# A transformer block on one core: the embedding's product moved to the prologue, roots on POOL, operands laid out in step

## The chip, the cores and the metric

The kernel runs on one core of a Trainium2 chip. The metric is the device time of one execution in microseconds (us), the median of several runs; less is better. The engines are named as in the profile: PE is TensorE (matmuls), DVE is VectorE, ACT is ScalarE, POOL is GpSimd, SP is SyncE, whose queue issues most of the DMAs. PEld is PE's loading of weights.

## The reference

One block on 512 tokens of width 1024, fp32 throughout. Cut to what matters:

```python
n1 = rmsnorm(x, g_mix)                       # x * rsqrt(mean(x*x) + 1e-6) * g
z = n1 @ w_in
y_ssm = s5_mixer(z[..., :512], ...)          # state-space mixer; its step sizes are dt = exp(log_dt)
y_nsa = nsa_mixer(z[..., 512:1024], z[..., 1024:1792], z[..., 1792:1816], ...)   # attention
merge = sigmoid(z[..., 1816:])
h = x + (merge_a * (y_ssm @ w_br_ssm) + merge_b * (y_nsa @ w_br_nsa)) @ w_out
h = h + conv_ffn(rmsnorm(h, g_ffn))          # up, depthwise conv, gelu(a) * b, down
gate = sigmoid(rmsnorm(h, g_ple) @ w_ple_gate)
h = h + gate * (p @ w_ple_proj)              # p is an input, 512 x 256
out = rmsnorm(h, g_final)
```

The embedding's product, `p @ w_ple_proj`, depends on inputs alone: it may be formed at any time before the last lines.

## The kernel before, in words

Every product is formed as three matmuls in a format that keeps the leading part of an fp32 number. An operand is split into a high part (a copy in that format, `copy`, L75) and a low part (what is left, a subtraction at L55; the pair is `split`, L78). `mm3` (L82 to L85) then sums high·high (L83), low·high (L84) and high·low (L85) in one PSUM bank. Tiles have 128 partitions; most matmuls write 128 x 512. Names ending in `h` and `l` are high and low parts; `wr` is a raw weight tile of 512 KB (three buffers), `wh` and `wl` its split (two buffers each).

The stages, by the time at which they stand in the trace before: the prologue (0 to 33 us); the state-space mixer and the projections `pj` of `n1` (from 33, with attention between and after them); the gated branches `glu` and `br`; the output product `wo` (to 404); the FFN's up products `ua` and `ub` (404 to 640) and its down products, formed with sums of blocks (`p`, to 770); last the PLE gate `pg` with the embedding's product, which also bears the name `pj` (767 to 824), the final norm and the output.

**The prologue.** SP loads the first tile of x, `g_mix`, the weights of the values and the attention's gates (`wv0`, `wv1`), the other three tiles of x, and two weights for u. For each tile of x the squares are summed (`squared`, L293; of the first tile ACT and DVE take half each), `rstd_of` (L121) turns the sum into a reciprocal root by eight dependent DVE operations of one or two columns (a first guess by bit pattern and three Newton steps), `x_scaled` multiplies by the root and by `gb`, the gain spread over partitions by a matmul with ones; `t_high` transposes on PE (`nt`) and copies the high part `n1h` on ACT, `t_low` subtracts to `n1l` on DVE; `v_passes` (L282) forms the values and gates (`vps`, 280 columns) in three passes of eight matmuls. The order of PE, ACT and DVE in this block is written by hand (the block under `manual_schedule`, L328). POOL's and SP's order is set by a scheduler; each engine's queue runs strictly in the order that it has been given.

POOL forms the mixer's parameters meanwhile: from `prm` (transposed parameters) the step sizes `dt`, an exponential of 22 small operations (`exp_of`, on POOL with a product and a sum as two instructions), then `lr`, `th`, `kk`, `fl`, a second exponential `rho`. DVE forms the angles `ang` and their sines later. POOL also clears the tiles `Z` and `CX` ahead of all this.

**The end.** `prepare` (L1278) is a generator whose steps are taken between products of the FFN's down stage: it loads p (`pin`), splits the weights of the gate, transposes p on PE (`ptr`, L1293) and splits it into `pTh`, `pTl`, loads `w_ple_proj` and splits it on POOL into `wph`, `wpl`. `embedded` (L1476) then forms one 128 x 512 tile of the embedding's product, six matmuls, in a PSUM bank; `gated` (L1482) forms the gate's product, a tanh on ACT (`sgt`), and on DVE adds gate times embedding to `hres`, the residual; ACT sums squares, POOL multiplies by the final gain, `rstd_of` gives the root, ACT and DVE scale the output.

Of the kernel before, what the change touches and what calls it, by code (L numbers as in the profile page):

```python
# [45 lines left out]
def hybrid_kernel(ctx: ExitStack, tc: tile.TileContext, A, out):  # L46
# [199 lines left out]
    xload(0)  # L246
    nc.sync.dma_start(grow, dr("g_mix", 0, [[D, 1], [1, D]]))
# [18 lines left out]
    ss4 = small("ss4", NQ + 1, 1)  # L266
# [25 lines left out]
    def squared(qt):  # L292
        S.activation(sq, xts[qt], AF.Square, accum_out=ss4[:, qt:qt + 1])  # L293
# [33 lines left out]

    with tc.manual_schedule(engines={mybir.EngineType.PE, mybir.EngineType.Activation, mybir.EngineType.DVE}):  # L328
        gbs = [bank("s", f"gb{i}") for i in range(2)]
        for ps, g in zip(gbs, halves(grow)):  # L330
            PE.matmul(ps, ones, g, start=True, stop=True)
        x0 = halves(xts[0])
        S.activation(sq[:, :512], x0[0], AF.Square, accum_out=ss4[:, 0:1])
        V.tensor_tensor_reduce(out=sq[:, 512:], in0=x0[1], in1=x0[1], scale=1.0, scalar=0.0, op0=MUL, op1=ADD,
                               accum_out=ss4[:, NQ:])
        pps = bank("t", "pps")
        for i in (2, 0, 1):
            PE.transpose(pps[:, i * 16:(i + 1) * 16], prow[:, i], ident[:NPAIR, :NPAIR])
        PE.transpose(pps[:, 48:52], drow, ident[:4, :4])
        copy(*wv(0, 0))  # L340
        copy(prm.rearrange("p a b -> p (a b)"), pps[:, :48])
        copy(dcol, pps[:, 48:52])
        x_scaled(0, rstd_of(ss4[:, 0:1], ss4[:, NQ:]))
        squared(1)
        t0 = t_high(0)
        V.tensor_copy(*wv(0, 1))
        v_passes(0, (0,))
        t_low(t0)
        v_passes(0, (1,))
        squared(2)  # L350
        squared(3)
        x_scaled(1, rstd_of(ss4[:, 1:2]))
        t1_ = t_high(1)
        v_passes(1, (0,))
        r = rstd_of(ss4[:, 2:4], n=2)
# [83 lines left out]
    exp_of(rho, lr, "e1", G)  # L439
# [158 lines left out]
    for t in (*ZZ[0], *CX[0], *ZZ[1], *CX[1]):  # L598
        G.memset(t, 0.0)
# [617 lines left out]
    with tc.manual_schedule(engines={mybir.EngineType.PE}):  # L1217
# [296 lines left out]
```

## Time and profile before

| | |
|---|---|
| median of 3 runs | 833.9 us (833.75 to 833.94) |
| the profiled execution: span | 833.0 us; some 0.9 us of a run lie outside the span |
| PE busy | 810.8 us, 97% of the span, 4535 instructions |
| DVE, ACT, POOL busy | 515.9, 391.3, 264.2 us |
| HBM | 75.54 MB read, 3.15 MB written |
| first projection matmul, last matmul | 33.0, 824.2 us |

How to read it: rows of a timeline give the start and the duration in us, engine, line, operation, the tile written, an arrow, the tiles read, and in brackets how long the engine was idle ahead of it and what ended that. Rows of windows give the stretch, its length, the busy time of PE, PEld, DVE, ACT and POOL with counts, the granted clock of PE as a share, the share of DMA engines that were busy, and GB/s. Rows with a count (x16) and three numbers are of one kind of instruction: least, median and greatest duration in ns. Matmuls overlap in their pipe: a 128 x 512 matmul lasts 389 ns, while the next starts after about 0.23 us.

### The profile page before, as it was taken

The numbers are of one execution on the slowest core, as the hardware profiler recorded it, in microseconds if no ns is written. First come the engines' busy times: TensorE is split into PE (matmuls) and PEld (weight loads), VectorE is DVE, ScalarE is ACT, GpSimd is POOL, SyncE is SP. The second block draws the span as 40 slices with busy tenths as digits, with TensorE's granted clock in tenths as the row PEclk, the third lists the DMA queues.
The fourth block names the chain that finished last, engine by engine and source line by source line (L and its number), as shares of the span: only waits on it lengthen the run. The fifth ranks groups of instructions, "written<-read, shape, count | busy, mean of one in ns | idle before, by whom it ended". The sixth has DMA issues, their size and how long they took to land. (4 is left out here: it accounts for less than half of the span.)

```text
span 833.0 us, 12232 instructions
## 1 busy us (share of the span) xinstructions
PE 810.8 (97%) x4535; PEld 678.6 (81%) x4535; DVE 515.9 (62%) x1067; ACT 391.3 (47%) x723; POOL 264.2 (32%) x320
## 2 busy tenths in 40 slices
PE   7999999999999999999999999999999999999995
PEld 5877888888888878888898888888888888877885
DVE  6899988377777641685454444445555755778643
ACT  4436553445777653434354444444444433546522
POOL 6585110124555533221033333333333000050311
PEclk9999999999999999999999999999999999999999
DMA  9653322422334413343053333333322553321011
GB/s 243 159 165 102 90 65 65 128 76 77 80 73 99 136 49 102 126 140 88 1 152 90 89 100 101 102 101 102 93 88 72 168 186 127 102 89 63 26 51 52
DMA packets 112001, 83.67 MB, mean 100 GB/s; under 512 B 9665, under 2 KB 97477, under 8 KB 111942
## 3 DMA queue, kind: packets, MB, share of 16 engines
q1 hardware_dynamic: 111262, 81.82, 33.9%
q10 hardware_dynamic: 680, 1.07, 0.3%
q8 instruction: 36, 0.59, 0.3%
q14 instruction: 23, 0.19, 0.1%
HBM read 75.54 MB, written 3.15 MB: 94 GB/s over the span
## 5 line engine op out<-in xcount | busy, mean ns | idle before, releaser
L55 POOL TENSOR_TENSOR wl<-wr,wh 128x1024 fp32r<-128x1024 f32 x39 | 93.6, 2400 | 246.9 <-ACT wh L76 228.9
L76 ACT ACTIVATE wh<-wr 128x1024 fp32r<-128x1024 f32 x92 | 97.3, 1059 | 95.8 <-issue 31.5
L55 DVE TENSOR_TENSOR wl<-wr,wh 128x1024 fp32r<-128x1024 f32 x53 | 68.4, 1291 | 49.2 <-ACT wh L76 49.2
L83 PE MATMUL pj<-n1h,wh 128*128 128x512 f32 x224 | 91.9, 410 | 0.4 <-ACT un L76 0.4
L85 PE MATMUL pj<-n1h,wl 128*128 128x512 f32 x224 | 88.8, 397 | 0.4 <-DVE wl L55 0.4
L84 PE MATMUL pj<-n1l,wh 128*128 128x512 f32 x224 | 88.8, 397 | 0.0
L64 DVE SCALAR_TENSOR_TENSOR cv<-ub,cvp,cv 128x511 f32<-128x511 f32 (+1 forms) x44 | 32.9, 748 | 65.5 <-ACT cv L1181 64.8
L84 PE MATMUL ua<-n2l,wh 128*128 128x512 f32 (+1 forms) x176 | 67.0, 381 | 0.4 <-DVE n2l L64 0.4
L83 PE MATMUL ua<-n2h,wh 128*128 128x512 f32 (+1 forms) x176 | 66.9, 380 | 0.2 <-ACT n2h L166 0.2
L83 PE MATMUL ub<-n2h,wh 128*128 128x512 f32 (+1 forms) x176 | 66.8, 379 | 0.0
L85 PE MATMUL ub<-n2h,wl 128*128 128x512 f32 (+1 forms) x176 | 66.8, 379 | 0.0
L84 PE MATMUL ub<-n2l,wh 128*128 128x512 f32 (+1 forms) x176 | 66.8, 379 | 0.0
L85 PE MATMUL ua<-n2h,wl 128*128 128x512 f32 (+1 forms) x176 | 66.7, 379 | 0.0
L85 PEld LDWEIGHTS pj<-n1h,wl 128*128 128x128 f32 x224 | 42.5, 190 | 10.3 <-DVE wl L55 1.1
L61 POOL TENSOR_SCALAR pr<-pr,su,gates 128x512 f32<-128x512 f32 (+1 forms) x64 | 38.4, 608 | 37.4 <-DVE su L877 36.3
L84 PEld LDWEIGHTS pj<-n1l,wh 128*128 128x128 f32 x224 | 42.6, 190 | 7.9 <-issue 0.6
L83 PEld LDWEIGHTS pj<-n1h,wh 128*128 128x128 f32 x224 | 42.5, 190 | 7.9 <-ACT un L76 0.6
L874 DVE CUSTOM_DVE_ANT_0 pr<-sps,maskb 128x512 f32<-128x512 f32 (+1 forms) x64 | 30.0, 487 | 18.8 <-PE sps L870 9.4
L55 DVE TENSOR_TENSOR pl<-ptp,ph 128x128 fp32r<-128x128 f32 (+1 forms) x64 | 31.1, 487 | 14.5 <-ACT ph L76 13.8
L76 ACT ACTIVATE ph<-ptp 128x128 fp32r<-128x128 f32 (+1 forms) x64 | 27.6, 433 | 25.7 <-PE ptp L885 25.0
L84 PEld LDWEIGHTS ua<-n2l,wh 128*128 128x128 f32 x176 | 33.1, 188 | 6.8 <-DVE n2l L64 0.6
L83 PEld LDWEIGHTS ua<-n2h,wh 128*128 128x128 f32 x176 | 33.1, 188 | 6.6 <-ACT n2h L166 0.5
(468 smaller groups left out, 2049.2 us busy)
## 6 DMA issues: line engine op xcount, KB each, us to landing
wr<-in_w_up_dram SPq DMA_DIRECT2D x44, 512.0 KB, 3.8
wr<-in_w_in_dram SPq DMA_DIRECT2D x28, 512.0 KB, 4.0
wr<-in_w_down_dram SPq DMA_DIRECT2D x12, 512.0 KB, 3.5
b<-in_w_down_dram SPq DMA_DIRECT2D x10, 512.0 KB, 4.0
QQ<-QT SPq DMA_DIRECT2D x16, 256.0 KB, 3.4
wr<-in_w_out_dram SPq DMA_DIRECT2D x8, 512.0 KB, 4.7
wr<-in_w_ple_gate_dram SPq DMA_DIRECT2D x8, 512.0 KB, 3.5
xall<-in_x_dram SPq DMA_DIRECT2D x4, 512.0 KB
```

What stands on the lines that cost most here:

```text
L55: e.tensor_tensor(o, a, b, op=op)
L61: e.tensor_scalar(o, a, s1, s2, op0=op0, op1=op1)
L64: e.scalar_tensor_tensor(o, a, s, b, op0=op0, op1=op1)
L76: S.activation(o, a, AF.Copy)
L83: PE.matmul(ps, lh, rh, start=start, stop=False)
L84: PE.matmul(ps, lh, rl, start=False, stop=False)
L85: PE.matmul(ps, ll, rh, start=False, stop=stop)
L874: V.tensor_tensor_reduce(out=pp, in0=ps[:, :w], in1=maskb[:, T - w:], scale=-(HD ** -0.5), scalar=3e38, op0=ADD, op1=ALU.min, accum_out=nb)
```

## The change

Its parts, in the order of the diff:

1. `rstd_of` has two POOL operations: the sum plus epsilon, then a power with exponent -0.5. The factor 1/1024 goes into the square's scale on ACT (`square`). All sums of squares lie in padded tiles (`sums`, `sums3`).
2. SP loads p first, then half of `w_ple_proj`, `g_mix`, x0, the other half, x1, `wv0`, x2, x3, `wv1`, the weights of u.
3. The prologue's hand-written order gets the whole embedding's product: p is transposed and split, `w_ple_proj` split, and eight tiles `eps` formed by `e_passes`, grouped by pass (first high·high of four tiles, so that it needs no low part) and put between the steps of x. ACT copies each tile to SBUF (`e_out`), SP writes it to a buffer in the HBM (`pjd`, 256 KB each).
4. The step sizes' exponential goes from POOL to DVE (14 operations there), the angles' reduction from DVE to POOL (12 operations of 128 x 128). `Z` and `CX` are cleared after the copy to `prow`. The squares of x0 are all ACT's.
5. `prepare` no longer transposes p nor splits `w_ple_proj`; it reads the eight tiles back from the HBM, and `gated` takes them from there. `embedded` is gone.
6. Small tiles are gathered or padded (`odds`, `sums`, `sums3`, two columns for `pe`) so that matmul operands start at the same place modulo 256 bytes of a partition: 224 bytes past a multiple in the build after, where the build before has 32, 160 and 224.

PE's queue at the program's start, before (`gb` is the gain spread, `nt` transposes of x, `vps` values):

```order
L331 MATMUL gb_141<-wv_110,ones 128x512
L331 MATMUL gb_142<-wv_110,ones 128x512
L338 MATMUL pps<-ident,prow 128x16 x3
L339 MATMUL pps<-ident,drow 128x4
L308 MATMUL nt<-ident,xall 128x128 x8
L282 MATMUL vps<-WV,n1h 128x280 x8
L282 MATMUL vps<-WV,n1l 128x280 x8
L308 MATMUL nt<-ident,xall 128x128 x8
L282 MATMUL vps<-WV,n1h 128x280 x8
L282 MATMUL vps<-WV,n1l 128x280 x8
L308 MATMUL nt<-ident,xall 128x128 x8
```

and after (`ptr` transposes of p, `eps` the embedding's tiles):

```order
L373 MATMUL ptr<-ident,pin 128x128 x8
L401 MATMUL pps<-ident,prow 128x16 x3
L402 MATMUL pps<-ident,drow 128x4
L384 MATMUL eps<-wh,pTs 128x512 x8
L411 MATMUL gb_192<-wv_112,ones 128x512
L411 MATMUL gb_193<-wv_112,ones 128x512
L384 MATMUL eps<-wl,pTs 128x512 x4
L384 MATMUL eps<-wh,pTs 128x512 x4
L384 MATMUL eps<-wl,pTs 128x512 x4
L384 MATMUL eps<-wh,pTs 128x512 x4
L343 MATMUL nt<-ident,xall 128x128 x8
L384 MATMUL eps<-wh,pTs 128x512 x4
```

The first transposes of x stand behind the transposes of p, 24 matmuls `eps` and `gb`; two more groups of 12 `eps` follow behind the first and the second tile's transposes. The value passes of the first tile, which stood right behind its transposes, now come behind those of the third.

DVE's root of the second tile of x, before (`ss` is the sum, `xall` x):

```order
L346 CAST WV<-wv_124 128x8x152
L55 TENSOR_TENSOR n1l<-nt,n1h 128x4x128 x2
L61 TENSOR_SCALAR rv_203<-ss_136 128x1
L61 TENSOR_SCALAR ry_204<-rv_203 128x1
L64 SCALAR_TENSOR_TENSOR rt_205<-ry_204,rv_203 128x1
L64 SCALAR_TENSOR_TENSOR ry_204<-rt_205,ry_204 128x1
```

and after, on POOL, in the midst of the mixer's parameters (`sums` holds the sums; `rv_277` and `ry_278` are the two operations of that root):

```order
L59 TENSOR_SCALAR gtFalse<-rd 128x16
L55 TENSOR_TENSOR at<-fl,mt 128x128
L55 TENSOR_TENSOR kk<-gtFalse,kk 128x16
L55 TENSOR_TENSOR ang<-kk,mt 128x128
L59 TENSOR_SCALAR gtFalse<-e1n 128x16
L61 TENSOR_SCALAR rv_277<-sums 128x1
L61 TENSOR_SCALAR aq<-ang 128x128
L59 TENSOR_SCALAR a_535<-ang 128x128
L55 TENSOR_TENSOR e1r<-gtFalse,e1x 128x16
L55 TENSOR_TENSOR ry_278<-rv_277,sums 128x1
```

The root's first half has 22 operations that follow from `dt` (rows from `lr` on, of which the first five shown are the last) ahead of it, and three other operations between its halves.

SP's queue at the start, before (`wv_110` holds `g_mix`, then the values' weights; `wv_124` their second part; `wr` weights of u):

```order
L244 DMA xall<-in_x_dram 128x1024
L247 DMA wv_110<-in_g_mix_dram 1x1024
L258 DMA wv_110<-in_w_in_dram 128x8x128
L258 DMA wv_124<-in_w_in_dram 128x8x152
L244 DMA xall<-in_x_dram 128x1024 x3
L183 DMA wr<-in_w_in_dram 128x8x128 x2
L263 DMA grow_113<-in_g_ffn_dram 8x128
```

and after (`wv_112` and `wv_134` are the two value tiles; the first two `wr` are halves of `w_ple_proj`):

```order
L251 DMA pin<-in_p_dram 128x4x256
L180 DMA wr<-in_w_ple_proj_dram 128x2x512
L261 DMA wv_112<-in_g_mix_dram 1x1024
L241 DMA xall<-in_x_dram 128x1024
L180 DMA wr<-in_w_ple_proj_dram 128x2x512
L241 DMA xall<-in_x_dram 128x1024
L270 DMA wv_112<-in_w_in_dram 128x8x128
L241 DMA xall<-in_x_dram 128x1024 x2
L270 DMA wv_134<-in_w_in_dram 128x8x152
L180 DMA wr<-in_w_in_dram 128x8x128
```

x0 stands behind p and half of `w_ple_proj`; x1 behind the other half, but ahead of the values' weights.

The diff, cut to its core:

```diff
     def rstd_of(ss, ss2=None, n=1):
-        v, y, t = (small(f"r{c}{n}", n) for c in "vyt")
-        ts(v, ss, 0.0 if ss2 is None else ss2, D * EPS, ADD, ADD)
-        ts(y.bitcast(I32), v.bitcast(I32), -0.5, FIRST, MUL, ADD)
-        for a in NEWTON[:3]:
...
+        v, y = (small(f"r{c}{n}", n) for c in "vy")
+        ts(v, ss, 0.0 if ss2 is None else ss2, EPS, ADD, ADD, G)
+        tt(y, v, minus[:, :n], ALU.pow, G)
         return y
...
+    def square(junk, x, acc):
+        S.activation(junk, x, AF.Square, scale=ROOT, accum_out=acc)
...
+    def p_turned(k):
+        ps = bank("t", "ptr")
+        for qt in range(NQ):
+            PE.transpose(ps[:, qt * P:(qt + 1) * P], pin[:, qt, k * P:(k + 1) * P], ident)
+        copy(pTs[:, 0, k], ps)
+        return ps
+
+    def e_passes(h2, qts, passes):
+        for n in passes:
+            for qt in qts:
+                if n == 0:
+                    eps[h2, qt] = bank(either(), "eps")
+                x, y = ((0, 0), (0, 1), (1, 0))[n]
+                for k in range(2):
+                    PE.matmul(eps[h2, qt], pTs[:, x, k, qt * P:(qt + 1) * P], wp[h2][y][:, k], start=n + k == 0,
+                              stop=n == 2 and k == 1)
+
+    def e_out(h2, qt):
+        t = stage[4 * h2 + qt]
+        if t is None:
+            t = pw.tile([P, 512], F32, name="pj", tag="mg")
+        copy(t, eps[h2, qt])
+        nc.sync.dma_start(pjd[h2, qt], t)
...
+        e_passes(0, range(4), (0,))
         gbs = [bank("s", f"gb{i}") for i in range(2)]
         for ps, g in zip(gbs, halves(grow)):
             PE.matmul(ps, ones, g, start=True, stop=True)
...
+        squared(0)
+        e_passes(0, range(2), (1, 2))
+        wp_tiles(1)
+        copy(wp[1][0], wpr[1])
+        exp_of(dt, prm[:, 2], "e0", V)
+        tt(wp[1][1], wpr[1], wp[1][0], SUB)
+        x_scaled(0, rstd_of(ss4[:, 0:1]))
+        e_out(0, 0)
+        e_out(0, 1)
+        squared(1)
+        e_passes(0, (2, 3), (1, 2))
+        e_out(0, 2)
+        e_out(0, 3)
+        t0 = t_high(0)
+        e_passes(1, range(2), (0, 1, 2))
+        x_scaled(1, rstd_of(ss4[:, 1:2]))
+        t_low(t0)
...
-            for k in range(2):
-                ps = bank(either(), "ptr")
...
-            for h2 in range(2):
-                raw = wraw("w_ple_proj", D, 0, h2 * 512, 2, 512)
-                for k in range(2):
-                    WP[k, h2] = [Slot(f"wp{x}", 1, F32R).t for x in "hl"]
-                    split(*WP[k, h2], raw[:, k], G)
...
+            for hf, qt in order:
+                pjs[hf, qt] = Slot("pj", 1).t
+                nc.sync.dma_start(pjs[hf, qt], pjd[hf, qt])
```

More of the change, by code (lines that the diff above doesn't have):

```diff
@@ L326, in u_split, with wp_tiles @@
             tt(uw[ct][1], uraw[ct], uw[ct][0], SUB)
-    with tc.manual_schedule(engines={mybir.EngineType.PE, mybir.EngineType.Activation, mybir.EngineType.DVE}):
+    pjd = pud.tile([2, NQ, P, 512], F32, name="pjd")
+    stage = [pin_[:, 1, :512], pin_[:, 1, 512:], pst[:, 0], pst[:, 1], None, None, pin_[:, 0, :512], pin_[:, 0, 512:]]
+    wp, eps = {}, {}
+    def wp_tiles(h2):
+        wp[h2] = [pw.tile([P, 2, 512], F32R, name=n, tag=n) for n in ("wh", "wl")]
+    def p_turned(k):
[19 more added lines that the diff above has]
+        nc.sync.dma_start(pjd[h2, qt], t)
+    with tc.manual_schedule(engines={mybir.EngineType.PE, mybir.EngineType.Activation, mybir.EngineType.DVE}):
+        wp_tiles(0)
+        pps_ = [p_turned(0)]
+        V.tensor_copy(wp[0][0], wpr[0])
+        pps_.append(p_turned(1))
+        pps = bank(either(), "pps")
+        for i in (2, 0, 1):
+            PE.transpose(pps[:, i * 16:(i + 1) * 16], prow[:, i], ident[:NPAIR, :NPAIR])
+        PE.transpose(pps[:, 48:52], drow, ident[:4, :4])
+        copy(prm.rearrange("p a b -> p (a b)"), pps[:, :48])
+        copy(dcol, pps[:, 48:52])
+        for k in range(2):
+            tt(pTs[:, 1, k], pps_[k], pTs[:, 0, k], SUB)
+        tt(wp[0][1], wpr[0], wp[0][0], SUB)
+        e_passes(0, range(4), (0,))
         gbs = [bank("s", f"gb{i}") for i in range(2)]
@@ L331, in hybrid_kernel @@
             PE.matmul(ps, ones, g, start=True, stop=True)
[L332 to L339, printed above, removed]
@@ L340, in hybrid_kernel @@
-        copy(*wv(0, 0))
[L341 to L355, printed above, removed]
@@ L1267, in onto @@
             tt(hres[:, qt, cs], hres[:, qt, cs], x, op, e)
-        WG, WP, pT, n3 = [], {}, {}, {}
+        WG, n3, pjs = [], {}, {}
+        order = [(hf, qt) for qp in range(2) for hf in range(2) for qt in (2 * qp, 2 * qp + 1)]
         def n3_(x, k, q, w):
@@ L1278, in prepare @@
         def prepare():
-            pin = pw.tile([P, NQ, PLE], F32, name="pin", tag="wr", bufs=3)
-            nc.sync.dma_start(pin, dr("p", 0, [[PLE, P], [P * PLE, NQ], [1, PLE]]))
             yield
@@ L1430, in hybrid_kernel @@
         sgn = [0]
-        ss = [pf.tile([P, 4], F32, name=f"ssf{qt}") for qt in range(NQ)]
-        def embedded(hf, qt):
-            qs_ = slice(qt * P, (qt + 1) * P)
-            pjs[hf, qt] = bank("s", "pj")
-            for k in range(2):
-                mm3(pjs[hf, qt], pT[k][0][:, qs_], pT[k][1][:, qs_], *WP[k, hf], k == 0, k == 1)
-        pjs = {}
+        ss = [sums3[:, 16 + 8 * qt:20 + 8 * qt] for qt in range(NQ)]
         def gated(hf, qt):
-            if (hf, qt) not in pjs:
-                embedded(hf, qt)
             pj = pjs[hf, qt]
@@ L1473, in gated @@
                         bass.AP(tensor=out.tensor, offset=out.offset + qt * P * D + i * 512, ap=[[D, P], [1, 512]]), o)
-        embedded(0, 0)
-        embedded(0, 1)
-        for n, (hf, qt) in enumerate([(hf, qt) for qp in range(2) for hf in range(2) for qt in (2 * qp, 2 * qp + 1)]):
+        for n, (hf, qt) in enumerate(order):
             if n in (2, 3):
```

167 lines of the change are left out of this document (91 added, 76 removed).

## The prediction

> **What bounds the kernel now.** I began with the page's busy times, then looked by windows for stretches in which TensorE is not full.
>
> ```profile
> PE 810.8 (97%) x4535; PEld 678.6 (81%) x4535; DVE 515.9 (62%) x1067; ACT 391.3 (47%) x723; POOL 264.2 (32%) x320
> 0.00:5.00 5.00, 0.10 (x1) 0.13 (x1) 0.37 (x1) 1.65 (x2) 4.36 (x26) 1.00 0.52 167
> 25.00:30.00 5.00, 4.06 (x32) 3.83 (x31) 4.36 (x5) 1.89 (x3) 4.33 (x7) 1.00 0.17 40
> 187.70:191.10 3.40, 3.40 (x10) 2.65 (x9) 3.40 (x7) 1.06 (x4) 2.83 (x2) 0.51 0.01 2
> 751.00:824.00 73.00, 72.06 (x358) 60.06 (x356) 46.55 (x108) 33.52 (x73) 14.11 (x10) 1.00 0.11 37
> 800.00:833.00 33.00, 24.50 (x131) 21.09 (x129) 13.04 (x38) 7.81 (x18) 6.58 (x6) 0.95 0.13 48
> ```
>
> The kernel is TensorE's queue from end to end: 97% busy. What it lacks lies at the start (x is awaited for 4.9 us), at the end (8.5 us after the last matmul) and in a few short waits. In 751 to 824, where the embedding's product stands now, TensorE has 72.06 of 73 us: a matmul taken out there shortens the run by its own time. The prologue is what has to pay for it, so I read TensorE's timeline there, with what released the first rows of other engines.
>
> ```profile
> 4.90 3.75 PE L331 MATMUL gb<-wv,ones 1*128 1x512 f32 x4 [4.90 <-DMA wv<-in_g_mix_dram]
> 8.91 1.97 PE L308 MATMUL nt<-ident,xall 128*128 128x128 f32 x8
> 22.83 1.14 PE L308 MATMUL nt<-ident,xall 128*128 128x128 f32 x8
> 24.84 1.19 PE L282 MATMUL vps<-WV,n1h 128*128 128x280 f32 x8
> 28.00 4.38 PE L282 MATMUL vps<-WV,n1h 128*128 128x280 f32 x32 [0.94 <-DVE WV L55]
> 33.01 0.48 PE L83 MATMUL pj<-n1h,wh 128*128 128x512 f32 x1
> 4.63 0.63 ACT L333 ACTIVATE sq<-xall 128x512 f32<-128x512 f32 x1 [0.56 <-DMA xall<-in_x_dram]
> 10.02 1.06 ACT L293 ACTIVATE sq<-xall 128x1024 f32<-128x1024 f32 x1 [0.73 <-DMA xall<-in_x_dram]
> ```
>
> The first projection matmul (`pj`, L83) starts at 33.01. From there on TensorE is nearly unbroken, so the change is settled by two numbers: how much later than 33.01 that matmul starts, and how much shorter the rest becomes. The transposes also show a slow start: 8 of them take 1.97 us at 8.91 and 1.14 at 22.83.
>
> **What the rest saves.** The embedding's product at the end, and the transposes of p that served it:
>
> ```profile
> 751.09 1.03 PE L1293 MATMUL ptr<-ident,pin 128*128 128x128 f32 x8
> 751.88 0.48 PE L83 MATMUL p<-wh,s14x 128*128 128x512 f32 x1
> 817.68 0.39 PE L85 MATMUL pj<-wph,pTl 128*128 128x512 f32 x1
> 818.37 0.39 PE L85 MATMUL pj<-wph,pTl 128*128 128x512 f32 x1
> L83 PE MATMUL pj<-wph,pTh x16: 389/389/478, 767.4 to 817.9; 128*128 128x512 f32 x16
> ```
>
> Between 817.68 and 818.37 lie three matmuls, 0.23 us each. Three passes of 16 are 48, so 11.0 us; the transposes hold the queue from 751.09 to 751.88, 0.8; changing tiles adds some 0.2. **12.0 us** go. What comes back is eight reads of 256 KB at a DMA share of 0.11, which I cost at nothing; if they came late, each would hold up the DVE step behind `sgt`, which isn't TensorE's.
>
> Beside it the splits of `w_ple_proj` on POOL go, and those of p on DVE:
>
> ```profile
> 747.51 1.71 POOL L55 TENSOR_TENSOR hres<-hres,su 128x512 f32<-128x512 f32 x1
> 748.02 2.35 DVE L55 TENSOR_TENSOR wl<-b,wh 128x512 fp32r<-128x512 f32 x2
> 749.82 0.50 PE L84 MATMUL p<-wl,s23x 128*128 128x512 f32 x1 [1.72 <-DVE wl L55]
> 752.56 0.69 DVE L55 TENSOR_TENSOR wl<-b,wh 128x512 fp32r<-128x512 f32 x1
> ```
>
> TensorE waits 1.72 us for a `wl` pair that takes 2.35 beside a POOL addition, where one alone takes 0.69. POOL is late there because `wpl` splits lie between its additions. With them gone I take **1.5 us** back (bounds 0 and 1.9).
>
> Roots: today eight dependent DVE operations, then two on POOL.
>
> ```profile
> 826.47 0.21 DVE L61 TENSOR_SCALAR rv<-ssf 128x1 f32<-128x1 f32 x1 [0.64 <-ACT sq L1459]
> 826.52 0.72 POOL L55 TENSOR_TENSOR hres<-hres,g 128x256 f32<-128x256 f32 x1 [1.98 <-ACT sq L1459]
> 828.43 0.72 ACT L1471 ACTIVATE xf<-hres,ry 128x512 f32<-128x512 f32 x1 [1.99 <-issue]
> 17.71 0.22 POOL L55 TENSOR_TENSOR lr<-lre,dt 128x16 f32<-128x16 f32 x1
> 23.35 0.25 POOL L59 TENSOR_SCALAR gtFalse<-e1n 128x16 f32<-128x16 f32 x1
> 411.55 0.39 PE L83 MATMUL ua<-n2h,wh 128*128 128x256 f32 x1 [0.24 <-ACT n2h L166]
> ```
>
> The DVE chain lasts 1.96 us (826.47 to 828.43). Nineteen small POOL operations last from 17.71 to 23.35, 0.30 each, so two are 0.6. No row shows a power; its near end is 0.30, its far end what an addition of 512 columns takes at its slowest above, 1.71. I take 0.3 to 0.4, since it writes one column as the nineteen write sixteen. At the tail POOL first does its `hres` (826.52, 0.72) and only then the root: 827.9 in place of 828.43, **0.4 us**. Ahead of the FFN some 1.2 us of chain go, of which TensorE shows a wait around 411: **0.7**. The SSM's tables lose twelve operations of DVE to POOL; two waits there are TensorE's, and with the queues between and behind them some 2.6 us, of which I take **1.5** (bounds 0 and 2.6):
>
> ```profile
> 62.05 0.50 PE L83 MATMUL pj<-n1h,wh 128*128 128x512 f32 x1 [0.36 <-ACT un L76]
> 69.89 1.16 PE L648 MATMUL wps<-Uc,WB 128*128 128x128 f32 x8 [0.89 <-ACT WB L76]
> ```
>
> Operands in step. In the build of before, `n2h`, `n2l` and `wh` start 32 bytes past a multiple of 256, `y`, `ys`, `mTh`, `w0h` 224 past, `oS` and `w1l` 160 past; after, all are 224 past. The rows, read by those phases:
>
> ```profile
> L83 PE MATMUL ua<-n2h,wh x176: 278/389/396, 404.7 to 641.9; 128*128 128x512 f32 x160, 128*128 128x256 f32 x16
> L83 PE MATMUL wo<-w0h,mTh x32: 387/389/499, 358.4 to 398.3; 128*128 128x512 f32 x32
> L84 PE MATMUL glu<-ys,wh x16: 390/394/398, 165.3 to 175.9; 128*128 128x512 f32 x16
> L85 PE MATMUL br<-oS,wl x32: 392/398/398, 337.0 to 358.2; 128*128 128x512 f32 x32
> ```
>
> Equal phases give 389 ns (32 with 32 in `ua`, 224 with 224 in `wo`), unequal ones 394 to 398. The unequal 512-wide ones are 48 of `glu`, 192 of `br` (in two tiles, `y` as `glu`) and, by half, some 100 of `wo`: 240 × 6 ns + 100 × 3 ns = **1.7 us** (bounds 0 and 2.5, and below nothing in a rival). [...]
>
> Together 12.0 + 1.5 + 0.4 + 0.7 + 1.5 + 1.7 = **17.8 us**.
>
> **What the prologue costs.** The walk of the new order, as an estimate. Before, four loads of 512 KB lie between x0 (4.6) and x1 (10.0), 1.3 to 1.8 each. Now p comes first (4.9), then half of `w_ple_proj` (6.2), x0 (7.5), the other half, x1 (10.1). TensorE: transposes of p to 6.6, pass 0 of four tiles, 8 matmuls at twice 0.23 while slow, 7.0 to 10.4; gb, its 3.75 at most, to 13.8.
>
> ```profile
> 9.35 0.81 DVE L346 CAST WV<-wv 128x1216 fp32r<-128x1216 f32 x1
> 12.89 0.14 DVE L61 TENSOR_SCALAR rv<-ss 128x1 f32<-128x1 f32 x1
> 14.65 1.41 DVE L64 SCALAR_TENSOR_TENSOR xall<-xall,ry,gb 128x512 f32<-128x512 f32 x2
> 26.64 1.38 POOL L55 TENSOR_TENSOR e1q<-gtFalse,e1r 128x16 f32<-128x16 f32 x1
> 27.87 1.24 DVE L55 TENSOR_TENSOR wl<-wr,wh 128x1024 fp32r<-128x1024 f32 x1
> ```
>
> DVE's queue: from 6.2 the cast, 0.8, two `pTs` 1.3 (each 0.69 as the subtraction at 752.56, overlapping a little), `wl` 1.2, to 9.5; the 14 dependent operations of the step sizes at 0.22 to 0.24 (eight take 12.89 to 14.65) to 12.8; `wl` to 14.0; x0 scaled 1.4, to 15.4. POOL, whose queue keeps its order, has 22 operations behind the step sizes ahead of the root of x1: 22 × 0.30, and one stretched by 1.1 beside `wl` (as 26.64 was beside DVE's splits, 1.38 where its like take 0.25) from 12.8: 20.6. The sum of squares of x1 is there at 17.4 (after gb eight matmuls to 15.6, ACT's second copy of `eps` to 16.2, squares 1.2), so the root is **held 3.2 us** by work that nobody needs yet, and three more rows stand between its two halves: 22.3. x1 is scaled at 23.7; without the hold, 19.4.
>
> From there a chain: transposes 0.9, two `n1h` 1.1, two `pj` copies 1.1, squares of x3 1.3, root and x2 scaled 2.6, `n1l` 1.3 and cast 0.8 ahead of the value passes: 9.1. Then TensorE is full: passes of tile 0 2.3, transposes 0.9, three tiles 6.6, the 32 low ones 4.4, small ones 0.6: 14.8. First `pj` at 23.7 + 9.1 + 14.8 = 47.6, against 33.0: **14.6 us later**. The floor is TensorE's own work at full speed: 11.9 for the embedding, 3.6 for 32 transposes (0.8 to 0.9 for eight, as from 751.09 to 751.88), 12.5 for 96 value matmuls at 0.13, 2.6 for gb and small ones, 30.6; with 4.9 for the start and 4 for the slow clock 39.5, a delay of 6.5. The far end is 19.7 (below).
>
> **Sum.** The profiled span is 833.0, the median 833.9, so 0.9 lies outside and stays. 833.0 − 17.8 + 14.6 = 829.8; with the 0.9, **830.7 us**. A difference under 0.2%, 1.7 us, counts as none.
>
> **Rivals.**
> - *POOL doesn't hold x1.* If its small operations go faster, or the step sizes come earlier, x1 is scaled at 19.4, `pj` starts at 43.3 and the time is 833.9 − 17.8 + 10.3 = 826.4; at the floor 822.6. For it: DVE's chain could start before 9.5. Against: 0.30 per operation is steady over 19 rows.
> - *Slower: TensorE's clock in the waits.* By the walk TensorE idles from about 20 to 24.4 and 28.3 to 31.6. The row 187.70 has clock 0.51 for 3.4 us though busy, so a drop costs 1.7 us. Two drops, and a slow start that lasts 3.4 us longer than in the walk (1.7 more), are 5.1: 835.8. It decides from a delay of 19.5 on. [...] Against: before shows none in the prologue after 17 us.
> - *224 is worse than 32.* Some 2,200 matmuls, the FFN's above all, by the build now run at 32 with 32. If 224 with 224 costs 3 ns more each, 6.6 us, and the 1.7 fall away: 839.0. It turns the sign from 0.7 ns on. Against: `wo` at 389.
> - *The steps do nothing to TensorE.* 394 might come from elsewhere in those stages; then 832.4, no change.
> - *The power is dear.* At 2 us in place of 0.35, the roots of x1 and x2, the one ahead of the FFN and the last one add 4 × 1.65 = 6.6: 837.3. No row speaks for or against.
>
> **Chances.** Forecast 0.43, POOL free 0.22, clock 0.13, 224 worse 0.06, steps idle 0.10, power dear 0.06. Faster: 0.22 and 0.38 of the forecast's, 0.60. Same: the steps' 0.10, 0.05 of the forecast, 0.05 of the clock, 0.20. Slower: 0.08, 0.06, 0.06, 0.20. The range reaches from 823.5 (POOL free, near the floor) to 838.0 (power dear) and leaves out the floor itself and most of the case of 224. The forecast's own range is 828.5 to 833.
>
> **What would show it.** First `pj` near 47.6, POOL's second root of x at 20.6 with its input at 17.4, an idle TensorE before the second set of transposes; no `pj` among the last 60 us, 12 us less there; `br` and `glu` at 389; a power at 0.3 us. I am wrong if `pj` starts before 43 or after 50, if `ua` leaves 389 ns, or if the last 80 us shrink by less than 11.

## The result, and the profile after

| | before | after |
|---|---|---|
| median of 4 runs | 833.9 us (833.8 to 834.6) | 838.8 us (837.9 to 840.5) |
| ratio | | 1.0062, 95% interval 1.0047 to 1.0076 |
| profiled execution: span | 833.0 | 837.1 |
| TensorE busy | 810.8 | 810.1 |
| first projection matmul | 33.0 | 50.3 |
| last matmul starts | 824.2 | 828.4 |

The change makes the kernel 4.9 us slower, where 830.7 and a range of 823.5 to 838.0 were forecast. The median lies 0.8 us above that range, and the sign is wrong.

One correction of the bookkeeping. The runs that came with the result list time and span together: 838.86 and 837.1 after, and in later runs of the kernel before 833.9 and 832.2. Some 1.7 us lie outside the span in both kernels. The 0.9 of the prediction was the difference between one profiled execution, 833.0 long, and the median of other runs. That execution was about 0.9 longer than most, since TensorE's clock fell in it from 187.7 to 191.1 (the window quoted there): the profiled run of e12 below, which differs only in one split near the end, has no such fall and gains 0.9 us on it across that stretch. Most runs of the kernel before have a mean clock of 0.996 to 0.998.

TensorE's timeline in the prologue after, with the rows on which the forecast was built (start, duration, engine, line, operation; in brackets the idle time ahead and what ended it):

```profile
4.89 1.94 PE L373 MATMUL ptr<-ident,pin 128*128 128x128 f32 x8 [4.89 <-POOL Z L665]
8.81 3.75 PE L384 MATMUL eps<-wh,pTs 128*128 128x512 f32 x8 [0.88 <-DVE wh L397]
12.50 3.77 PE L411 MATMUL gb<-wv,ones 1*128 1x512 f32 x4
16.20 2.07 PE L384 MATMUL eps<-wl,pTs 128*128 128x512 f32 x4
18.07 1.91 PE L384 MATMUL eps<-wh,pTs 128*128 128x512 f32 x4
19.78 1.38 PE L384 MATMUL eps<-wl,pTs 128*128 128x512 f32 x4
21.00 1.08 PE L384 MATMUL eps<-wh,pTs 128*128 128x512 f32 x4
33.72 1.71 PE L343 MATMUL nt<-ident,xall 128*128 128x128 f32 x8 [3.82 <-DVE n1l L55]
35.11 2.21 PE L296 MATMUL vps<-WV,n1h 128*128 128x280 f32 x8
50.27 0.48 PE L83 MATMUL pj<-n1h,wh 128*128 128x512 f32 x1
```

The first `pj` is 17.3 us later than before; 14.6 were forecast. The first pass runs at 0.47 us a matmul, and groups of four `eps` take 2.07, 1.91 and 1.38 us before they take 1.08 from 21.0 on: TensorE is slow until about 20.4, not until 13.8. (The trace's first record of the clock, full speed, stands at 20.40; windows ahead of it show 1.00. That the slow rows are a halved clock is inferred from the first experiment, where the same 1.91 us stands beside a recorded clock near one half.) Then it waits 3.82 us, for the third tile of x, which DVE scales from 31.66 on, and last for `n1l` of the second tile, which DVE has behind that. The matmuls after the wait (1.71, 2.21) are slow again: the granted clock is 0.50 from 34.05 to 37.46.

Who held x, on ACT, DVE and POOL (one fence, rows in that order):

```profile
6.15 2.52 DVE L397 CAST wh<-wr 128x1024 fp32r<-128x1024 f32 x1 [6.15 <-DMA wr<-in_w_ple_proj_dram]
23.85 1.41 DVE L64 SCALAR_TENSOR_TENSOR xall<-xall,ry,gb 128x512 f32<-128x512 f32 x2 [6.79 <-POOL ry L55]
31.66 1.41 DVE L64 SCALAR_TENSOR_TENSOR xall<-xall,ry,gb 128x512 f32<-128x512 f32 x2 [5.20 <-POOL ry L55]
19.17 0.60 ACT L76 ACTIVATE pin<-eps 128x512 f32<-128x512 f32 x1 [8.63 <-PE eps L384]
20.51 1.05 ACT L129 ACTIVATE sq<-xall 128x1024 f32<-128x1024 f32 x1
28.65 1.07 ACT L129 ACTIVATE sq<-xall 128x1024 f32<-128x1024 f32 x1
21.18 0.25 POOL L59 TENSOR_SCALAR gtFalse<-e1n 128x16 f32<-128x16 f32 x1
21.73 0.24 POOL L61 TENSOR_SCALAR rv<-sums 128x1 f32<-128x1 f32 x1 [0.30 <-ACT sq L129]
23.24 0.58 POOL L55 TENSOR_TENSOR ry<-rv,sums 128x1 f32<-128x1 f32 x1
30.90 0.72 POOL L55 TENSOR_TENSOR ry<-rv,sums 128x2 f32<-128x2 f32 x1
```

DVE waits 6.79 us for x1's root and 5.20 for that of x2 and x3. POOL's root of x1 starts at 21.73 after 0.30 us in which POOL itself waits for ACT's squares. ACT squares x1 at 20.51 because it had waited 8.63 us for an `eps` tile that stands ahead in its order; x1 lay in SBUF by then, as the first experiment shows. POOL's queue was through with the work ahead of that root at 21.43, so ACT ended last by 0.2 us only.

The second place is the third of the four sets of transposes of `xn`, near 792. The expectations below call it the last transposes.

```profile
789.71 2.39 POOL L55 TENSOR_TENSOR wg1l<-wr,wg1h 128x1024 fp32r<-128x1024 f32 x1
789.78 4.01 DVE L59 TENSOR_SCALAR xn<-hres,ry 128x512 f32<-128x512 f32 x2 [0.60 <-POOL ry L55]
792.53 0.30 PE L160 MATMUL nt<-ident,xn 128*128 128x128 f32 x1 [1.35 <-DVE xn L59]
793.85 0.98 PE L160 MATMUL nt<-ident,xn 128*128 128x128 f32 x7 [1.01 <-DVE xn L59]
```

and the same place in the kernel before, where TensorE does not wait:

```profile
776.50 2.40 POOL L55 TENSOR_TENSOR wg1l<-wr,wg1h 128x1024 fp32r<-128x1024 f32 x1 [2.45 <-ACT wg1h L76]
780.55 0.88 DVE L59 TENSOR_SCALAR xn<-hres,ry 128x512 f32<-128x512 f32 x2
781.17 1.29 PE L163 MATMUL nt<-ident,xn 128*128 128x128 f32 x8
```

Two scalings of xn take 4.01 us beside POOL's split (and POOL's product with the gain behind it, at 792.05) and 0.88 without; TensorE waits 1.35 and 1.01. In the kernel before a step of the root on DVE takes 2.29 us beside the same split (at 776.62; its like 0.16 at 776.03), and TensorE, with two of the embedding's tiles more to do ahead of that set, does not wait for it. The prologue's cast of 2.52 us stood beside POOL's clearing of `Z` and `CX`. By what way POOL's work could lengthen DVE's, no run here shows.

Where the 4.1 us between the two profiled spans come from, by TensorE's starts of the same matmuls in both traces: first `pj` +17.3; from there to the output product (396.8 before, 410.8 after) −3.3, of which 0.9 are the clock drop of before's profiled execution; across the transposes ahead of the FFN −0.7; to the wait for `wl` (749.8 and 762.9) −0.2; transposes of p −0.9; eight embedding tiles of 1.36, −10.9; the wait for xn 2.4 and a second wait for `wl` 0.5, +2.9; tail −0.1.

### The profile page after: what moved, and what is told of

Read it like the earlier page. It is cut to its first block, busy times and chain, and to the rows that moved or that the text cites. A ratio compares the mean times of both kernels' runs of the same rounds, so it can differ in the third digit from the quotient of the medians.

```text
span 837.1 us, 12176 instructions
## 1 busy us (share of the span) xinstructions
PE 810.1 (97%) x4535; PEld 678.1 (81%) x4535; DVE 499.4 (60%) x959; ACT 393.5 (47%) x728; POOL 270.1 (32%) x332
## 4 chain that ended last, share of the span: by engine, by line
PE 83%; DVE 8%; ACT 3%; issue 2%; DMA 1%; POOL 0%; POOLq 0%; SPq 0%; ACTq 0%; DVEq 0%
PE pj L83 5%; PE pj L85 5%; PE pj L84 5%; PE ua L84 5%; PE ua L85 5%; PE ua L83 5%; PE ub L84 5%; PE ub L83 5%; PE ub L85 5%; PE sps L936 2%; PE dn L84 2%; PE dn L85 2%; PE dn L83 2%; PE ptp L951 2%; DVE wl L55 2%
## 5 line engine op out<-in xcount | busy, mean ns | idle before, releaser
L55 DVE TENSOR_TENSOR wl<-wr,wh 128x1024 fp32r<-128x1024 f32 x55 | 72.0, 1309 | 48.7 <-ACT wh L76 48.6
L61 POOL TENSOR_SCALAR pr<-pr,su,odds 128x512 f32<-128x512 f32 (+1 forms) x64 | 38.5, 612 | 33.7 <-DVE su L943 32.5
L55 DVE TENSOR_TENSOR pl<-ptp,ph 128x128 fp32r<-128x128 f32 (+1 forms) x64 | 31.1, 487 | 14.2 <-ACT ph L76 13.8
L84 PEld LDWEIGHTS ub<-n2l,wh 128*128 128x128 f32 x176 | 33.1, 188 | 6.3
L85 PEld LDWEIGHTS ua<-n2h,wl 128*128 128x128 f32 x176 | 33.1, 188 | 6.3
```

What stands on the lines that cost most here:

```text
L55: e.tensor_tensor(o, a, b, op=op)
L61: e.tensor_scalar(o, a, s1, s2, op0=op0, op1=op1)
L84: PE.matmul(ps, lh, rl, start=False, stop=False)
L85: PE.matmul(ps, ll, rh, start=False, stop=stop)
```

## The experiments

Theory A, formed from the two traces: the loss is ACT's order in the prologue, which puts x1's and x3's squares behind embedding tiles made late by a slow TensorE, and the split beside the second norm, which the embedding's tiles used to cover. The rivals: the prologue is bound by TensorE, so that holds are hidden; POOL's queue holds x1, as predicted; the roots on POOL are the loss.

**e1: squares early.** On ACT, x1 to x3 are squared before the first embedding tile is copied; the scheduler then puts POOL's roots ahead of the parameters too.

```diff
+        for qt in (1, 2, 3):
+            squared(qt)
         e_out(0, 0)
         e_out(0, 1)
-        squared(1)
...
-        squared(2)
...
-        squared(3)
...
```

> The kernel after with one edit: ACT squares x1, x2 and x3 before it copies the first embedding tiles, where it sat idle for 8.6 us; the scheduler then also puts both roots ahead of the mixer's parameters on POOL. Theory A (x1 and x2/x3 are held by the order on ACT and POOL, which put them behind embedding tiles that slow matmuls made late): x2 and x3 are scaled by about 25, TensorE's wait of 3.8 us before the third tile's transposes and the clock drop in it go, the first pj starts near 45.5 and not 50.3; time about 834. Rival B (the prologue is bound by TensorE's own slow matmuls, the holds are hidden): first pj stays within 1 us of 50.3 and the time at 838.5.

Measured: 833.0 us median of 10 (829.5 to 834.8), 5.8 less than after; ratio to before 0.998 (0.9963 to 0.9997). Its profiled run, at 829.5 the fastest:

```profile
11.03 1.06 ACT L129 ACTIVATE sq<-xall 128x1024 f32<-128x1024 f32 x1 [0.34 <-DMA xall<-in_x_dram]
15.38 1.06 ACT L129 ACTIVATE sq<-xall 128x1024 f32<-128x1024 f32 x1 [0.15 <-DMA xall<-in_x_dram]
14.55 2.72 DVE L64 SCALAR_TENSOR_TENSOR xall<-xall,ry,gb 128x512 f32<-128x512 f32 x4
14.07 1.19 PE L384 MATMUL eps<-wl,pTs 128*128 128x512 f32 x4
16.60 1.91 PE L384 MATMUL eps<-wl,pTs 128*128 128x512 f32 x4
26.72 1.04 PE L343 MATMUL nt<-ident,xall 128*128 128x128 f32 x8
41.61 0.48 PE L83 MATMUL pj<-n1h,wh 128*128 128x512 f32 x1
15.60:19.00 3.40, 3.40 (x10) 2.62 (x10) 1.67 (x3) 1.90 (x4) 2.63 (x12) 0.54 1.20 297
```

x1 is squared at 11.0, as soon as it lands, both x0 and x1 are scaled in one go at 14.55, and TensorE waits for neither the second nor the third set of transposes. First `pj` at 41.6, in an execution 3.5 us under the median. Theory A's time, 834, holds for the median; the rival that the holds are hidden falls. The spread of 5 us was not expected, and the runs fall in two groups, 829.5 to 831.9 and 834.1 to 834.8: the four `eps` at 14.07 are fast, those at 16.60 slow again. Since POOL's roots moved as well, this run does not tell ACT's share of the gain from POOL's.

**e13: POOL alone freed.** The mixer's parameters on POOL go behind all roots of x; ACT's order stays as in the kernel after.

```diff
+        root_at = last(mybir.EngineType.Pool)
...
+    behind.enter_context(tc.issue_after(root_at))
```

> The kernel after with POOL's mixer parameters put behind the three roots of x, so that POOL is free when a sum of squares comes; the orders of ACT, DVE and TensorE unchanged. The prediction's theory (POOL holds x1's root by 3.4 us): x1 is scaled at 22 in place of 25.3, first pj 47, time 836. Theory A (ACT's order holds it just as long, POOL adds 0.3 us and 0.9 between the root's halves): x1 scaled at 24.3, x2 some 0.8 us earlier, first pj near 49, time about 838 or, if the parameters come late, more.

Measured: 840.2 us (836.9 to 842.5), not faster than after. In its profiled run, the fastest, POOL waits for ACT's sum:

```profile
18.28 0.23 POOL L61 TENSOR_SCALAR rv<-sums 128x1 f32<-128x1 f32 x1 [7.09 <-ACT sq L129]
19.18 1.41 DVE L64 SCALAR_TENSOR_TENSOR xall<-xall,ry,gb 128x512 f32<-128x512 f32 x2 [3.28 <-POOL ry L55]
```

POOL is idle for 7.09 us and starts the moment that ACT is done. From the end of the squares to x1 scaled it now takes 2.4 us and not 3.6: what POOL's queue added was 1.2. So ACT holds x1 with POOL free, and the prediction's account, in which POOL alone holds it, is refuted for the traced execution of after. It is not refuted for all: the sum comes at 18.2 here, and not at 21.7, since TensorE's matmuls were fast from about 12.7 in this run. With such a start POOL's queue would hold x1 some 3 us, about as predicted: in e2 below, which starts as fast and has no roots on POOL, the sum is there at 18.3 and POOL is through the same 22 operations at 21.2. No run shows that case with the roots on POOL, and none frees ACT alone. Of the 5.0 us by which e13 was ahead of the kernel after at the third transposes, 3.2 are lost again by 75 us, where TensorE waits 1.23 us for the mixer's `un` and 1.54 for `Z` (0.42 for `Z` in after); that the parameters, which come late here, are the cause is argued, not shown. So the time alone says little.

**e2: roots on DVE.** The kernel after with the eight Newton operations in `rstd_of`, as before.

```diff
-        ts(v, ss, 0.0 if ss2 is None else ss2, EPS, ADD, ADD, G)
-        tt(y, v, minus[:, :n], ALU.pow, G)
+        ts(v, ss, 0.0 if ss2 is None else ss2, D * EPS, ADD, ADD)
+        ts(y.bitcast(I32), v.bitcast(I32), -0.5, FIRST, MUL, ADD)
+        for a in NEWTON[:3]:
...
```

> The kernel after with its roots as before, eight Newton operations on DVE, all else unchanged. Theory A (the root on POOL costs in the prologue 1.2 us of x1 between its halves and in the last stage lets POOL's split start beside DVE's scaling of xn): the wait of 2.4 us before the last transposes falls to about 1, the prologue's first pj comes about 1 us earlier, the wait ahead of the FFN is 0.7 longer; time about 837. Rival B (roots on POOL are a gain of about 1.5 us): 840. Either way: if the 0.87 us by which the time outside the span grew come from the power, the difference of time and span falls from 1.75 to 0.9.

Measured: 841.2 us (840.6 to 842.9), 2.4 slower than after: rival B of this run, by more than it said. Ahead of the transposes near 792 TensorE falls 3.8 us behind the kernel before, 2.6 in the kernel after. Behind them the profiled execution of e2 has a clock drop (794.5 to 797.9, 1.6 us) that the one of after lacks, and the first `pj` comes 1.8 us earlier, with TensorE fast from 12.9 on: the size of 2.4 holds chance of the clock as well. Time less span is 1.7 here too, so the power has no part in that.

**e3 and e3b: roots on POOL alone**, in the kernel before; e3b differs only in the padding of one small tile.

```diff
-    minus = cp.tile([P, 2], F32, name="minus")
+    minus = cp.tile([P, 64], F32, name="minus")
```

> The kernel before with the roots alone moved to POOL (sum plus epsilon and a power; factor 1/1024 in the squares). Theory A (a power takes 0.55 to 0.7 us and the POOL root as a whole 0.9, against 1.9 on DVE, where TensorE waits for it: ahead of the FFN, before the last transposes, at the tail): 833.8 - 0.7 - 1 = about 832. Rival B (POOL's queue and its split beside xn eat the gain): 833.8 or more.

> As e3, roots on POOL in the kernel before, but with the tile of -0.5 padded to 256 bytes, so that every operand of the three-pass matmuls starts where it does before (in e3 the 714 of the down stage stood at 64 with 32 in place of 32 with 32, and its matmuls drifted by 0.45 us in each 15 us). Theory A (2.3 of e3's 2.7 us are that drift): 834.3, no change within 0.7 us. Rival B (the roots on POOL cost it): 836.5.

Measured: e3 836.7 us (ratio 1.0031, 1.0019 to 1.0043), e3b 833.25 (0.9992, 0.9983 to 1.0001). A tile of 8 bytes, with the tiles that it replaces, cost 2.5 us against the kernel before; padded, the roots on POOL are worth about nothing there, and in the kernel after up to 2.4. In the build of e3 the down stage's matmuls have operands at 64 and 32 past a multiple of 256; its 128 x 512 matmuls last 395 ns where they last 389 in e3b, and TensorE falls 2.8 us behind e3b between 650 and 745.

**e9: out of step.** The kernel after without its padding.

```diff
-    sums = cp.tile([P, 8], F32, name="sums")
+    sums = cp.tile([P, 6], F32, name="sums")
...
-    odds = pa.tile([P, 128], F32, name="odds")
+    odds = pa.tile([P, 104], F32, name="odds")
...
-        pe = small("pe", 1, 2)
+        pe = small("pe")
...
-    sums3 = pf.tile([P, 64], F32, name="sums3")
+    sums3 = pf.tile([P, 84], F32, name="sums3")
```

> The kernel after with its padding taken out (sums of 6 columns, gates and masks of 104, the later sums of 84, pe in four buffers). In this build some 970 of the matmuls of three passes have operands whose starts differ modulo 256 (the down stage's 32 with 224 above all), 1728 both at 32 and 240 both at 224. Theory A (unequal starts cost 5 to 6 ns each, equal ones nothing, whichever they are): 838.8 + 5.3 = 844, with 394 ns or so for the down stage's matmuls. Rival B (starts do nothing, glu and br were slow for another reason): 838.8 within 0.5.

Measured: 841.5 us (840.5 to 842.4), 2.7 more than after: theory A's sign, half its size. But of the 2.8 us between the two profiled executions only some 1.0 lies in such matmuls; 1.7 is a clock drop behind the transposes near 792 (last row of the second view), which the profiled execution of after, with the same waits ahead of it, does not have. By kind of matmul (least, median, greatest duration in ns), first after, then e9:

```profile
L83 PE MATMUL glu<-ys,wh x16: 389/389/395, 182.0 to 192.4; 128*128 128x512 f32 x16
L85 PE MATMUL br<-oS,wl x32: 388/389/389, 351.1 to 371.7; 128*128 128x512 f32 x32
L84 PE MATMUL br<-y,wh x32: 389/393/398, 234.7 to 286.6; 128*128 128x512 f32 x32
L84 PE MATMUL dn<-wl,ffp x96: 389/389/504, 661.6 to 726.6; 128*128 128x512 f32 x96
```

```profile
L83 PE MATMUL glu<-ys,wh x16: 394/394/394, 182.1 to 192.8; 128*128 128x512 f32 x16
L84 PE MATMUL dn<-wl,ffp x96: 392/394/394, 662.1 to 727.4; 128*128 128x512 f32 x96
L85 PE MATMUL dn<-wh,ffp x96: 388/388/394, 662.3 to 727.6; 128*128 128x512 f32 x96
795.77:799.18 3.41, 3.41 (x10) 2.67 (x9) 2.26 (x5) 2.06 (x6) 0.79 (x1) 0.50 0.00 0
```

`glu` and `br<-oS` come down to 389 in step and `glu` goes back to 394 out of it. Of the down stage's three passes only some pay (394, 388): 0 to 5 ns by pass. So a start out of step has a cost, shown best by e3 against e3b; the share of e9's 2.7 us that is this cost is about 1.0 and the rest is open. `br<-y` stays at 393 though in step, so there it is something else. By what way a start out of step costs these few ns, no run here shows.

**e4 and e10: the product left out.** The kernel before without the embedding's product, its loads, transposes and splits (tiles of x are read in its place, so the output lacks it); e10 has besides the last low part of the gate's weights split on DVE.

```diff
-        embedded(0, 0)
-        embedded(0, 1)
...
+                nc.sync.dma_start(pjs[hf, qt], dr("x", qt * P * D + hf * 512, [[D, P], [1, 512]]))
```

> The kernel before with the embedding's product left out (the eight tiles are read from x in its place, so the output lacks it); nothing is added to the prologue. It measures by itself what taking the product out of the end is worth. By my sum of the prediction 12.0 + 1.5 us: 820.4. By theory A (the three embedding tiles ahead of the last transposes were cover for the second norm's chain): some 2.4 us less is saved, 822.5 to 823.

> The kernel before with the product left out of the end, as in the earlier run that gained 5.7 us, and with the last low part of the gate's weights on DVE. Theory A (of the 4.4 us that TensorE waited before the last transposes there, the larger part is POOL's split beside DVE's root and scaling, the rest the bare chain without its cover): the wait falls to 2 us or less, time about 826. Rival B (the wait is the chain of residual, squares, root and scaling alone): 828.2.

Measured: e4 828.2 us (0.993, 0.9915 to 0.9945), e10 825.7 (0.9901, 0.9888 to 0.9914). Taking out 12 us of matmuls, with nothing put in the prologue, gains 5.7. The transposes of `xn` in question, in e4 and in e10:

```profile
780.78 2.06 PE L163 MATMUL nt<-ident,xn 128*128 128x128 f32 x8 [3.67 <-DVE xn L59]
```

```profile
779.19 1.29 PE L163 MATMUL nt<-ident,xn 128*128 128x128 f32 x8 [2.63 <-DVE xn L59]
```

TensorE waits 3.67 us for the second norm in e4, and its transposes then take 2.06 at a clock that has fallen (0.50 from 780.5 to 783.9, a loss of 1.7 us); 2.63 and 1.29 in e10. The wait, the drop and some 0.6 us lost near 710 are what separates 5.7 from 12. Theory A's split of the wait holds in direction, but the bare chain is larger than I expected. It is the chain with the root on DVE; with the root on POOL, and the split out of its way, TensorE does not wait for it at all, as the next run shows.

**e5 and e12: that split alone**, in the kernel after and in the kernel before.

```diff
-                    wload("w_ple_gate", D, 2 * c * P, 512, 2, 512, (V, G)[c % 2],
+                    wload("w_ple_gate", D, 2 * c * P, 512, 2, 512, (V, G, V, V)[c],
```

> The kernel after with the last low part of the gate's weights on DVE, behind the scaling of xn, in place of POOL. Theory A (DVE's scaling of xn took 4.0 us and not 0.9 because POOL's split of 1024 columns, which stands right behind the root, ran beside it): xn is 0.9 us again, the wait of 2.4 us before the last transposes falls to under 0.3, time about 836.5. Rival B (that wait is the chain of residual, squares and root, which lost its cover of embedding matmuls): the wait stays at 2 us or more and the time at 838.5.

> The kernel before, whole, with only the last low part of the gate's weights moved from POOL to DVE: the edit that gained 2.8 us in the kernel after and 2.5 with the product left out. Theory A (in the kernel before the embedding's tiles ahead of the last transposes cover that chain, so that its slowness costs nothing): 833.8 within 0.7 us. Rival B (the split is a fault of its own, that the kernel before pays too): 831.3.

Measured: e5 836.0 us (834.9 to 836.6), 2.8 less than after; e12 833.45 (0.9996, 0.9987 to 1.0006), no change. In e5:

```profile
789.89 0.89 DVE L59 TENSOR_SCALAR xn<-hres,ry 128x512 f32<-128x512 f32 x2 [0.60 <-POOL ry L55]
791.13 1.04 PE L160 MATMUL nt<-ident,xn 128*128 128x128 f32 x8
```

The scaling is back at 0.89 and TensorE's wait is gone. The same edit is worth 2.8, 2.5 and 0 us: with the embedding's tiles in front of the transposes the chain's slowness is hidden, without them it is TensorE's. Of the 2.5 some 1.3 is e4's clock drop, which goes with the shorter wait.

**e6 and e11: together, and the gain first.** e6 is e1 with the split of e5; e11 moves TensorE's gain matmuls ahead of the embedding's first pass besides.

```diff
+        gbs = [bank("s", f"gb{i}") for i in range(2)]
+        for ps, g in zip(gbs, halves(grow)):
+            PE.matmul(ps, ones, g, start=True, stop=True)
         copy(prm.rearrange("p a b -> p (a b)"), pps[:, :48])
...
         e_passes(0, range(4), (0,))
-        gbs = [bank("s", f"gb{i}") for i in range(2)]
...
```

> The two edits together: squares of x1 to x3 early on ACT, and the last low part of the gate's weights on DVE behind the scaling of xn. If the two losses are separate places (prologue, second norm), their gains add: 838.8 - 5.8 - 2.8 = 830.2, with the same two groups of runs as with the squares alone, near 827 and 831.5. If one is hidden by the other, it stays at 833.

> The kernel of e6 with TensorE's four gain matmuls (one row of weights) moved ahead of the embedding's first pass, where TensorE waits 0.9 to 1.5 us. Theory A (the clock rises only after a stretch of 3.4 us full of wide matmuls; the gain's matmuls, in the midst of the first passes, spoil one or two such stretches, which is why e1 had full clock at 12.2, lost it again from 15.6 to 19.0, and e6 had it only from 20.6): passes then run unbroken from 11, full clock comes once, between 14 and 18, and stays; the first pj falls between 41.5 and 43.5, the time between 826 and 828 with a spread under 4 us. Rival B (the clock's start is set by chance alone): same spread of 826 to 834 and median 829.

Measured: e6 829.0 us (826.3 to 833.6), e11 827.3 (826.0 to 828.0), ratio 0.9919 (0.9904 to 0.9933). The gains add, within the spread, and both beat the two kernels. TensorE in e6 and in e11:

```profile
12.59 3.78 PE L411 MATMUL gb<-wv,ones 1*128 1x512 f32 x4
18.17 1.91 PE L384 MATMUL eps<-wh,pTs 128*128 128x512 f32 x4
21.52 1.08 PE L384 MATMUL eps<-wh,pTs 128*128 128x512 f32 x4
44.66 0.48 PE L83 MATMUL pj<-n1h,wh 128*128 128x512 f32 x1
```

```profile
7.37 3.76 PE L405 MATMUL gb<-wv,ones 1*128 1x512 f32 x4
14.63 1.91 PE L384 MATMUL eps<-wl,pTs 128*128 128x512 f32 x4
17.54 1.09 PE L384 MATMUL eps<-wl,pTs 128*128 128x512 f32 x4
41.55 0.48 PE L83 MATMUL pj<-n1h,wh 128*128 128x512 f32 x1
```

With the gain in the midst, TensorE is busy from 8.9 and slow until about 21.4; with the gain first, wide matmuls run from 11.05 and are fast from about 17, and the spread shrinks from 7.3 us (six runs) to 2.0 (four runs). Full clock, first `pj`, time and spread lie where theory A of that run put them; its rule for the clock is an inference from e1 and e6 that no run isolates.

## Why the prediction was wrong, by its steps

- **"A matmul taken out there shortens the run by its own time": the step that failed first.** It rested on 72.06 busy us of 73 in that window. The matmuls were as dear as reckoned (8 tiles of 1.36 and 0.9 for the transposes, 11.8), but the two tiles ahead of the third set of transposes of `xn` were what filled TensorE while residual, squares, root and scaling of the second half ran. In the kernel after some 2.4 us came back there as a wait (3.67 in e4, and 1.7 more by the clock drop behind it). e5 and e12 show the cover: the same edit gains 2.8 us without it and nothing with it. A full engine shows no waits because something covers them; I asked of each other edit what hid it, and not what the product itself was hiding.
- **The prologue, 14.6: measured 17.3, with the place right and the holder wrong.** x1 scaled at 25.3 (23.7 reckoned) and the wait before the third set at 29.9 to 33.7 (28.3 to 31.6) came as walked. But the hold was put down to POOL, with the sum at 17.4; the sum came at 21.65 and POOL was free at 21.43. That x1's time was nearly met is luck: the sum came 4.3 us later than reckoned, and POOL's queue added 1.2 us instead of 4.3. The two numbers that moved the sum: the cast, 2.52 and not 0.8, beside POOL's clearing of tiles, and TensorE slow until 20.4 and not 13.8. (In before two loads, not four, lie between those of x0 and x1; x1 landed at 11.0 in e1, not at 10.1.) That ACT would stand idle from 10.5 to 19.2, behind a copy of a tile, with x1 landed, was in the quoted order and not weighed: I counted ACT's copies as 1.1 us of work ahead of the squares, not as a wait for TensorE.
- **The rival of the clock came true in part**: one drop behind a wait (0.50 from 34.05 to 37.46, 1.7 us), not two, and a slow start that lasted 6.6 us longer than in the walk (3.3 us), nearly twice what that rival had. It was priced at 5.1 us and given 0.13; it did not act alone. That a wait brings a drop was an estimate that no row of before shows; in after one drop follows a wait of 3.82 us, and in e13 slow matmuls (eight `vps` in 2.20 us at 30.14) follow one of 3.17.
- **The wait for `wl` near 750, 1.5: about nothing.** TensorE waits 1.32 us there after, and 0.48 at 766.24, against 1.72 before:

```profile
755.69 5.09 POOL L55 TENSOR_TENSOR hres<-hres,su 128x512 f32<-128x512 f32 x3 [1.23 <-DVE su L55]
759.57 1.77 DVE L55 TENSOR_TENSOR wl<-u,wh 128x512 fp32r<-128x512 f32 x1
761.39 0.50 PE L84 MATMUL p<-wl,s23x 128*128 128x512 f32 x1 [1.32 <-DVE wl L55]
```

  POOL's additions run beside DVE's stretched split here too; the splits of `w_ple_proj` that went were not the cause. e4, where they went as well, waits as long (1.28 and 0.48 us).
- **In step, 1.7: right in kind**, 389 ns in `glu`, `br<-oS` and `wo`; `br<-y` gained little, which leaves 48 × 5 + 96 × 6 + 100 × 3 ns = 1.1 us, an estimate by count. The rivals "224 is worse" (`ua` and `dn` at 389) and "the steps do nothing" (e3 against e3b, the rows of e9) fall.
- **Roots.** A power takes 0.55 to 0.72 us, and 1.12 beside DVE's work at 788.62, not 0.3 to 0.4. The 0.7 ahead of the FFN came (TensorE's lag to before falls by 0.68 at that set of transposes); the tail's 0.4 was 0.1. In the kernel before the whole is worth 0.5 us, not clear of the noise (e3b).
- **The SSM's 1.5** can't be told apart: of the 3.3 us saved between the first `pj` and the output product, 0.9 is the clock drop of the other profile and some 1.1 the operands in step, which leaves 1.3 or so for it and for whatever else moved there.
- **The sum** −17.8 + 14.6 = −3.2 became +4.9, a difference of 8.1: 2.7 in the prologue, 2.4 by the lost cover, 1.4 at 750, 0.2 in the SSM, 0.6 in step, 0.3 at the tail, 0.2 in the product itself and 0.4 lost near 710, for which no run shows a cause, are 8.2. What stays open is the size of chance in it: runs of one kernel lie 5 to 6 us apart in e1 and e13, and clock drops, such as the 1.7 us that e9's profiled run has behind 792 and that of after has not, are part of that by estimate.

## What to carry to other kernels

Before taking work off a busy engine, ask which chain of other engines runs behind it up to that engine's next input; only what is left over that chain is gained. When work is put into a gap, look at every in-order queue that its results pass, and do there first what is already landed. An edit that is worth nothing in one version can be worth 2.8 us in the next, so a part is to be tried again after the others.

## What the runs showed of the hardware that I had not expected

- TensorE came to full speed at different times in kernels with nearly the same first matmuls. Four matmuls with one row of weights (`gb`, 3.8 us) stand in the midst of wide ones in after and its variants; there full speed came at 20.4 to 21.6 (after, e5, e6, e9), or at 12.7 to 12.9 and stayed through the embedding's passes (e2, e13), or at 11.9 and went again from 15.3 to 18.8 (e1). With them first it came at 16.9 and stayed (e11). The drops of before and after last 3.41 us each (from 187.70 and from 34.05), and in after the drop starts 13.65 us, four times as much, behind the record of full speed at 20.40. In the last 3.41 us ahead of full speed TensorE is busy throughout, without any `gb`, in before (13.6 to 17.0), after (17.0 to 20.4), e11 (13.5 to 16.9) and, but for 0.1 us, e1 (8.5 to 11.9); with 0.4 us of `gb` in e13 (9.3 to 12.7). Behind stretches as long and as full that hold 1.0 us of it (10.1 to 13.5 in e11), or 1.1 (10.2 to 13.6 in after), TensorE was still slow: four `eps` took 1.91 us at 14.63 in e11. Whether the one row of weights makes the difference, no run isolates.
- The start of an operand modulo 256 bytes was worth up to 6 ns of 389 for many 128 x 512 matmuls whose two operands differ (395 against 389 in the down stage of e3 and e3b); a tile of 8 bytes in e3 cost 2.5 us, most of it by this (e3 falls 2.8 us behind e3b between 650 and 745).
- A cast of 128 x 1024 on DVE took 2.52 us beside POOL's clearing of tiles (2.00 in e1); one of 128 x 1216 without it took 0.79 at 34.17.
